# A two-layer gated-linear-attention and latent-attention trunk: x laid out transposed, its norm moved onto the products, and two projections in 512-column blocks

## The chip, the cores and the metric

One Trainium2 chip, one core. The metric is the device time of one execution of the whole program in microseconds (us). Two kernels are compared by the median of several executions on the same chip; one more execution of each is run under the hardware profiler, and its trace is what this document reads.

The engines are named as the profile names them: PE is the matrix engine (PEld its weight loads), DVE the vector engine, ACT the scalar engine, POOL the general one, SP the engine whose queue issues most of the transfers.

## What is computed

512 positions of width 2048 in float32 pass through two layers. Only the parts at the edges of the change are given.

```python
def rms_norm(x, g, eps):                       # over the last axis
    return x * rsqrt(mean(x * x) + eps) * g

def layer0(x):                                 # gated linear attention, 4 heads
    h = rms_norm(x, pre_norm)
    q, k, v, gate, gk_low = split(h @ w_in)    # 1024, 1024, 2048, 2048, 16 columns
    log_a = log_sigmoid(gk_low @ w_gk2 + b_gk) / 16
    o = chunked_scan(q, k, v, log_a)           # o is then normed per head
    return x + rms_norm((rms_norm(o, g) * silu(gate)) @ w_out, post_norm)

def layer1(x):                                 # latent attention, 16 heads
    h = rms_norm(x, pre_norm)
    c_q, c_kv, k_rope, gate = split(h @ w_in)  # 512, 512, 64, 2048 columns
    ...                                        # c_q and c_kv are normed, projected, attended
    return x + rms_norm((attention * silu(gate)) @ w_out, post_norm)
```

## The kernel before

**Numbers.** Every large product is made from three products of rounded parts: an operand is split into a high part (`..._hi`, rounded by ACT or DVE) and the rest (`..._lo`, by DVE), and `mm3` (L123) issues hi·hi, lo·hi and hi·lo into one accumulator. So each weight chunk goes through a load (`chunk_load`, SP's queue), a split (`chunk_split`) and the products. Where a gain of a norm belongs to the layer's input, the split multiplies the weights by it: per 128 weight rows one ACT instruction (L118) and one DVE instruction (L119).

**Tiles.** The 512 positions are four row tiles `s` of 128, the 2048 inputs 16 tiles `k`. `act_hi` and `act_lo` hold the normed input with the inputs on the partitions. In `block_t` the weights are the stationary operand and the 512 positions stream; in `block_s` (through `part_s`) a 128x128 tile of the activations is stationary and the weight columns stream, 256 or 512 of them per product.

**The start** (`start`, L224). x comes in rows, four tiles of 128 positions. For each tile: sums of squares on ACT, the norm's factor, the row times the factor on DVE (L330), sixteen 128x128 transposes on PE in four groups (L333), the split into `act_hi` and `act_lo` (L174, L175). The first head's values are made in two passes of 256 columns: the first inside `start`, row tile by row tile with weights that stay, the second in `gla` (L346). Then `gk_low` (L378), the decays, and the blocks of q, k, gate and v of each head.

**Between the layers** (`between`, L611) each row tile of the first output is normed, added to x, stored, normed again and transposed by the same `rows_to_act`. The first latent, c_q, is also made in two passes of 256 columns. For the first, weights of 14 of the 16 tiles `k` are split ahead (`cq_ahead`, L688) and those of the last two in `mla` (L649); so work for PE is there as each row tile becomes ready.

**Order.** The program is written as above, and a scheduler with a model of its own moves instructions on each engine; every engine then works through its list in order. Transfers of SP's queue start in order, and each buffer waits for its last reader: three raw weight buffers, four split ones, two accumulators for transposes (`ps_t`).

Of the kernel before, what the change touches and what calls it, by code (L numbers as in the profile page):

```python
# [49 lines left out]
R_BGK, R_GON, R_GQA, R_GKV, R_PRE = 0, 8, 12, 16, 20  # L50
NROWS = 36
# [19 lines left out]
class Trunk:  # L71
# [152 lines left out]
    def start(self):  # L224

        nc, a, cp = self.nc, self.a, self.cp
        xs = a["x"][0]
        xt = [self.slot(f"g{s}", [P, D], F32, f"x{s}") for s in range(ST)]
        rows = self.tmp([KT, P], F32, "gain_rows")
        cf = cp.tile([P, P + 1], F32, name="cf")  # L230
        for g in range(4):
            c = slice(g * 512, (g + 1) * 512)
            nc.sync.dma_start(xt[0][:, c], xs[0:P, c])
            if g == 0:
                nc.scalar.dma_start(cf, a["consts"])
                nc.scalar.dma_start(rows, a["l0_pre_norm"].rearrange("(r c) -> r c", c=P))
        self.ident, self.invf = cf[:, 0:P], cf[:, P:P + 1]
        self.eps = cp.tile([P, 1], F32, name="eps")
        nc.vector.memset(self.eps, EPS)
        self.junk = cp.tile([P, 512], BF16, name="junk")  # L240
        pt = self.pss.tile([P, 512], F32, tag="sc", name="gain_t")
        nc.tensor.transpose(pt[:, 0:KT], rows, self.ident[0:KT, 0:KT])
        self.g_in = cp.tile([P, KT], F32, name="g_in0")
        nc.vector.tensor_copy(self.g_in, pt[:, 0:KT])
        w = a["l0_gla_w_in"]
        load = lambda i: self.chunk_load(w, 4 * i, 4, [(GV0, 256)])
        raws = [load(0)]
        nc.sync.dma_start(xt[1], xs[P:2 * P, :])
        raws.append(load(1))
        nc.sync.dma_start(xt[2], xs[2 * P:3 * P, :])  # L250
        raws.append(load(2))
        ws = []
        self.v_ps = [self.acc(f"v_acc{s}", s == 3) for s in range(ST)]
        for s in range(ST):
            parts = self.st.tile([P, 4], F32, tag="parts", name="parts", bufs=2)
            for g in range(4):
                self.sumsq(xt[s][:, g * 512:(g + 1) * 512], parts[:, g:g + 1])
            rstd = self.rstd_of(self.total(parts, "x_ssq"), D, "x_rstd")
            self.rows_to_act(s, xt[s], rstd)
            for i in range(4):  # L260
                if s == 0:
                    if i == 3:
                        raws.append(load(3))
                        nc.sync.dma_start(xt[3], xs[3 * P:4 * P, :])
                    ws.append(self.chunk_split(raws[i], 4 * i, self.g_in, hi_on=nc.vector if i % 2 else None))
                self.part_s(s, 4 * i, ws[i], self.v_ps, slice(0, 256), self.act_hi, self.act_lo, KT)

    def constants(self):
# [11 lines left out]
        rows = self.tmp([P, P], F32, "rows")  # L280
        for r0, name in ((R_BGK, "l0_gla_b_gk"), (R_GON, "l0_gla_g_onorm"),
                         (R_GQA, "l1_mla_g_qa"), (R_GKV, "l1_mla_g_kva"), (R_PRE, "l1_pre_norm")):
            n = a[name].shape[0] // P
            q.dma_start(rows[r0:r0 + n, :], a[name].rearrange("(r c) -> r c", c=P))
        self.ones = cp.tile([P, P], F32, name="ones")
        nc.gpsimd.memset(self.ones, 1.0)
# [3 lines left out]
        pt = self.pst.tile([P, 512], F32, tag="pt", name="gcols")  # L290
        nc.tensor.transpose(pt[:, 0:NROWS], rows[0:NROWS, :], self.ident[0:NROWS, 0:NROWS])
        self.gcol = cp.tile([P, NROWS], F32, name="gcol")
        nc.vector.tensor_copy(self.gcol, pt[:, 0:NROWS])
        with self.tc.issue_after(self.last_norm.ins):
            self.trig(posi, self.invf)
# [43 lines left out]
    def gla(self):  # L339
# [3 lines left out]
        self.vh, self.vl, self.sg = None, None, [None] * GH  # L343
        self.constants()
        self.v_begin()
        self.block_s(w, GV0 + 256, 256, 256, self.v_ps, hi, lo, KT, evac=self.v_evac, gain=self.g_in)  # L346
# [3 lines left out]
        for h in range(GH):  # L350
# [3 lines left out]
            if h:  # L354
                ps = [self.acc(f"v_acc{s}", s == 3) for s in range(ST)]
                self.v_begin()
                self.block_s(w, GV0 + h * GDV, 512, 0, ps, hi, lo, KT, evac=self.v_evac, gain=self.g_in)
# [17 lines left out]
    def v_evac(self, s, ps):  # L375
        self.split_from(ps, self.vh[s], self.vl[s])

    def gk_low(self):  # L378
        nc, v, a = self.nc, self.nc.vector, self.a
        raw = self.tmp([P, KT, 2 * GRANK], F32, "gkl_raw")  # L380
        sc = raw[:, :, GRANK:]
        raw = raw[:, :, 0:GRANK]
        nc.gpsimd.dma_start(raw, a["l0_gla_w_in"][:, GL0:GL0 + GRANK].rearrange("(k p) n -> p k n", p=P))

        wl = self.slot("g1", [P, KT, 3 * GRANK], FR, "gkl_w")
        nc.gpsimd.memset(wl[:, :, GRANK:2 * GRANK].bitcast(F32), 0.0)
        v.tensor_tensor(sc, raw, self.g_in[:, :, None].to_broadcast([P, KT, GRANK]), ALU.mult)
        nc.scalar.copy(wl[:, :, 0:GRANK], sc)
# [254 lines left out]
    def mla(self):  # L643
# [286 lines left out]
```

## Time and profile before

| | us |
|---|---|
| median of 3 executions | 1505.87 (1505.53 to 1507.59) |
| the profiled execution | 1507.5 |
| its span, first to last instruction | 1505.7 |
| PE busy in the span | 1485.8 |
| DVE busy | 742.5 |
| ACT busy | 657.1 |

The span is what the trace covers; 1.8 us of the execution lie around it. A matmul's record lasts longer than the distance to the next one, because matmuls overlap; what a stream of them takes is read from the distances between starts. "Idle before" gives how long an engine stood still ahead of an instruction, and what it waited for. An idle engine costs nothing where another one sets the end.

### The profile page before, as it was taken

The numbers are of one execution on the slowest core, as the hardware profiler recorded it, in microseconds if no ns is written. First come the engines' busy times: TensorE is split into PE (matmuls) and PEld (weight loads), VectorE is DVE, ScalarE is ACT, GpSimd is POOL, SyncE is SP. The second block draws the span as 40 slices with busy tenths as digits, with TensorE's granted clock in tenths as the row PEclk, the third lists the DMA queues.
The fourth block names the chain that finished last, engine by engine and source line by source line (L and its number), as shares of the span: only waits on it lengthen the run. The fifth ranks groups of instructions, "written<-read, shape, count | busy, mean of one in ns | idle before, by whom it ended". The sixth has DMA issues, their size and how long they took to land.

```text
span 1505.7 us, 19208 instructions
## 1 busy us (share of the span) xinstructions
PE 1485.8 (99%) x7490; PEld 1266.6 (84%) x7490; DVE 742.5 (49%) x1337; ACT 657.1 (44%) x1250; POOL 35.0 (2%) x72
## 2 busy tenths in 40 slices
PE   7999999999999999999999999999999999999998
PEld 6988888888888888888889888888888899888886
DVE  6544653355436445434355443333577677853234
ACT  6542642254225424333244443344566667742221
POOL 2100000000000000100011000000000000000000
PEclk9999999999999999999999999999999999999999
DMA  6423223322331323434252333333222111234223
GB/s 222 122 71 98 71 87 95 101 82 80 90 110 57 98 84 119 134 111 134 91 188 92 101 98 98 98 99 91 74 74 74 50 50 55 83 126 168 98 91 119
DMA packets 113867, 149.91 MB, mean 100 GB/s; under 512 B 17580, under 2 KB 66976, under 8 KB 112368
## 3 DMA queue, kind: packets, MB, share of 16 engines
q1 hardware_dynamic: 110176, 136.86, 29.9%
q0 software_dynamic: 3424, 11.75, 2.4%
q8 instruction: 58, 0.95, 0.3%
q14 instruction: 33, 0.27, 0.1%
q10 hardware_dynamic: 176, 0.07, 0.0%
HBM read 140.08 MB, written 8.59 MB: 99 GB/s over the span
## 4 chain that ended last, share of the span: by engine, by line
PE 95%; DVE 2%; ACT 1%; DMA 1%; issue 0%; SPq 0%; DVEq 0%; ACTq 0%
PE acc L125 11%; PE acc L127 11%; PE acc L126 11%; PE yo_acc L125 8%; PE yo_acc L126 8%; PE yo_acc L127 8%; PE v_acc L127 5%; PE v_acc L125 5%; PE v_acc L126 5%; PE o_t L127 1%; PE o_t L126 1%; PE q_acc L127 1%; PE q_acc L126 1%; PE q_acc L125 1%; PE o_t L125 1%; PE pt L882 1%
## 5 line engine op out<-in xcount | busy, mean ns | idle before, releaser
L125 PE MATMUL acc<-act_hi,w_hi 128*128 128x512 f32 x768 | 299.7, 390 | 0.0
L126 PE MATMUL acc<-act_hi,w_lo 128*128 128x512 f32 x768 | 299.2, 390 | 0.0
L127 PE MATMUL acc<-act_lo,w_hi 128*128 128x512 f32 x768 | 298.9, 391 | 0.0
L119 DVE SCALAR_TENSOR_TENSOR w_lo<-w_raw,g_in,w_hi 128x512 fp32r<-128x512 f32 (+1 forms) x208 | 139.7, 707 | 206.7 <-ACT w_hi L118 206.6
L118 ACT ACTIVATE w_hi<-w_raw,g_in 128x512 fp32r<-128x512 f32 (+1 forms) x200 | 128.1, 689 | 242.9 <-PE acc L127 166.6
L127 PEld LDWEIGHTS acc<-act_lo,w_hi 128*128 128x128 f32 x768 | 144.2, 188 | 30.7 <-issue 0.7
L125 PEld LDWEIGHTS acc<-act_hi,w_hi 128*128 128x128 f32 x768 | 144.2, 188 | 30.4 <-issue 0.7
L126 PEld LDWEIGHTS acc<-act_hi,w_lo 128*128 128x128 f32 x768 | 144.3, 188 | 29.8
L111 DVE TENSOR_TENSOR w_lo<-w_raw,w_hi 128x1024 fp32r<-128x1024 f32 x64 | 78.4, 1225 | 166.7 <-ACT w_hi L110 166.6
L110 ACT CAST w_hi<-w_raw 128x1024 fp32r<-128x1024 f32 x64 | 67.3, 1051 | 168.4 <-PE yo_acc L126 156.8
L125 PE MATMUL yo_acc<-w_hi,act_hi 128*128 128x512 f32 x352 | 137.5, 391 | 0.0
L126 PE MATMUL yo_acc<-w_hi,act_lo 128*128 128x512 f32 x352 | 137.1, 390 | 0.0
L127 PE MATMUL yo_acc<-w_lo,act_hi 128*128 128x512 f32 x352 | 137.1, 391 | 0.0
L119 DVE SCALAR_TENSOR_TENSOR w_lo<-w_raw,gcol,w_hi 128x512 fp32r<-128x512 f32 (+1 forms) x98 | 64.6, 699 | 106.1 <-ACT w_hi L118 105.9
L126 PE MATMUL v_acc<-w_hi,act_lo 128*128 128x512 f32 (+1 forms) x320 | 112.2, 352 | 0.0
L118 ACT ACTIVATE w_hi<-w_raw,gcol 128x512 fp32r<-128x512 f32 (+1 forms) x98 | 61.4, 677 | 115.5 <-PE acc L127 83.8
L125 PE MATMUL v_acc<-w_hi,act_hi 128*128 128x512 f32 (+1 forms) x320 | 111.5, 351 | 0.2 <-ACT act_hi L174 0.2
L127 PE MATMUL v_acc<-w_lo,act_hi 128*128 128x512 f32 (+1 forms) x320 | 110.7, 350 | 0.0
L127 PEld LDWEIGHTS yo_acc<-w_lo,act_hi 128*128 128x128 f32 x352 | 66.1, 188 | 14.0 <-issue 0.2
L125 PEld LDWEIGHTS yo_acc<-w_hi,act_hi 128*128 128x128 f32 x352 | 66.1, 188 | 13.8 <-issue 0.2
L126 PEld LDWEIGHTS yo_acc<-w_hi,act_lo 128*128 128x128 f32 x352 | 66.1, 188 | 13.4
L125 PEld LDWEIGHTS v_acc<-w_hi,act_hi 128*128 128x128 f32 x320 | 61.4, 192 | 8.0 <-ACT act_hi L174 0.6
(300 smaller groups left out, 2688.9 us busy)
## 6 DMA issues: line engine op xcount, KB each, us to landing
w_raw<-in_l_gla_w_in_dram SPq DMA_DIRECT2D x64, 512.0 KB, 3.7
w_raw<-in_l_mla_w_in_dram SPq DMA_DIRECT2D x47, 512.0 KB, 3.7
w_raw<-in_l_gla_w_in_dram SPq DMA_DIRECT2D x64, 256.0 KB, 3.0
w_raw<-in_l_gla_w_out_dram SPq DMA_DIRECT2D x32, 512.0 KB, 3.7
w_raw<-in_l_mla_w_out_dram SPq DMA_DIRECT2D x32, 512.0 KB, 3.6
pw_raw<-in_l_mla_w_kvb_dram SPq DMA_DIRECT2D x64, 128.0 KB, 2.3
xo<-in_x_dram POOLq DMA_DIRECT2D x16, 256.0 KB, 6.0
x1d<-yo SPq DMA_DIRECT2D x4, 1024.0 KB, 5.8
```

Of the source, the lines that this page charges most:

```text
L110: nc.scalar.copy(hi, raw)
L111: nc.vector.tensor_tensor(lo, raw, hi.bitcast(F32), ALU.subtract)
L118: nc.scalar.activation(hi[:, kk, :], raw[:, kk, :], AF.Copy, scale=g)
L119: nc.vector.scalar_tensor_tensor(lo[:, kk, :], raw[:, kk, :], g, hi[:, kk, :].bitcast(F32), ALU.mult, ALU.subtract)
L125: t.matmul(out, lh, rh, start=start, stop=False)
L126: t.matmul(out, ll, rh, start=False, stop=False)
L127: t.matmul(out, lh, rl, start=False, stop=stop)
L882: te.transpose(pt[:, o:o + P], probs[i][:, j * P:(j + 1) * P], self.ident)
```

## The change

Host side, x is given a second time, transposed (`xt`, inputs by positions), and the six small gain vectors as one 128x52 array `gains`. In the kernel:

- `start` loads `xt` by tiles `k` beside the first head's value weights in 512 columns. x times its gain is split straight into `act_hi` and `act_lo` (`x_split`); the factor of the norm is left out there. Sums of squares are collected per position over the tiles `k` in `x_ssq`; four narrow products and one 512-column product with ones (`x_norm`) make the factors, per row tile (`rcol`) and along the free axis (`rrow`).
- The weights of layer 0 are split without a gain. The factor is applied to the products: to v in `v_evac`, to q and k in `qk_block`, to the gate in `silu`, to `gk_low`'s 16 rows.
- Five products of zeros (`zeros`) go to PE ahead of everything else.
- c_q is made in one pass of 512 columns: seven tiles `k` split ahead, the eighth in `mla`, the other eight as a block.
- The transposes of gains and small vectors go; `restart` and the scratch of `gk_low` change places.

```diff
@@ start
-        xt = [self.slot(f"g{s}", [P, D], F32, f"x{s}") for s in range(ST)]
...
-        load = lambda i: self.chunk_load(w, 4 * i, 4, [(GV0, 256)])
...
-        for s in range(ST):
...
-            self.rows_to_act(s, xt[s], rstd)
-            for i in range(4):
...
-                self.part_s(s, 4 * i, ws[i], self.v_ps, slice(0, 256), self.act_hi, self.act_lo, KT)
+        self.gcol = cp.tile([P, NCOLS], F32, name="gcol")
+        nc.scalar.dma_start(self.gcol, a["gains"])
+        load_x(0, 1)
+        raws = [self.wp.tile([P, 2, 512], F32, tag="raw", name="w_raw", bufs=3)]
+        for k in range(2):
+            nc.sync.dma_start(raws[0][:, k, :], w[k * P:(k + 1) * P, GV0:GV0 + 512])
+            if k == 0:
+                load_x(1, 1)
...
+        v.memset(self.junk, 0.0)
+        pz = self.pss.tile([P, 512], F32, tag="sc", name="zeros")
+        for _ in range(5):
+            nc.tensor.matmul(pz, self.junk[:, 0:P], self.junk, start=True, stop=True)
...
+        for k0 in range(0, KT, 2):
+            if k0:
+                load_x(k0, 2)
+                raws.append(self.chunk_load(w, k0, 2, [(GV0, 512)]))
+            x = xs[k0 // 4][:, k0 % 4:k0 % 4 + 2, :]
+            if k0:
+                self.x_split(k0, 2, x)
+                wt = self.chunk_split(raws[-1])
...
+            for i in range(2):
...
+                    nc.scalar.activation(sq, x[:, i, :], AF.Square)
+                    v.tensor_tensor(ssq, ssq, sq, ALU.add)
...
+            if k0 + 2 == KT:
+                self.x_norm(ssq)
+            for s in range(ST):
...
+                    self.part_s(s, k0, wt, ps, slice(0, 512), self.act_hi, self.act_lo, KT)
+
+    def x_split(self, k0, nk, x):
+        for i in range(nk):
+            k = k0 + i
+            g = self.gcol[:, R_IN + k:R_IN + k + 1]
+            self.nc.scalar.activation(self.act_hi[:, k, :], x[:, i, :], AF.Copy, scale=g)
+            self.nc.vector.scalar_tensor_tensor(self.act_lo[:, k, :], x[:, i, :], g,
+                                                self.act_hi[:, k, :].bitcast(F32),
+                                                ALU.mult, ALU.subtract)
+
+    def x_norm(self, ssq):
...
+        for s in range(ST):
+            nc.tensor.matmul(pc[:, s:s + 1], ssq[:, s * P:(s + 1) * P], self.ones[:, 0:1],
+                             start=True, stop=True)
...
+        self.norm_mm = nc.tensor.matmul(pn, self.ones, ssq, start=True, stop=True)
@@ constants
-        with self.tc.issue_after(self.last_norm.ins):
+        with self.tc.issue_after(self.last_evac.ins):
             self.trig(posi, self.invf)
@@ gla
-        self.block_s(w, GV0 + 256, 256, 256, self.v_ps, hi, lo, KT, evac=self.v_evac, gain=self.g_in)
@@ qk_block
+            n = self.tmp([P, S], F32, "qk")
+            v.tensor_tensor(n, ps, self.rrow, ALU.mult)
@@ silu
+        if r is not None:
+            nc.vector.tensor_tensor(g, ps, r, ALU.mult)
+            ps = g
@@ mla
-        self.cq_w.append(self.chunk(w, KT - 2, 2, [(MQ0, 256)], self.g_in))
+        self.cq_w.append(self.chunk(w, KT // 2 - 1, 1, [(MQ0, 512)], self.g_in))
         for s in range(ST):
             for i, wt in enumerate(self.cq_w):
-                self.part_s(s, 2 * i, wt, ps, slice(0, 256), hi, lo, KT)
-        self.block_s(w, MQ0 + 256, 256, 256, ps, hi, lo, KT, evac=self.latent_evac, gain=self.g_in)
+                self.part_s(s, i, wt, ps, slice(0, 512), hi, lo, KT)
+        self.block_s(w, MQ0, 512, 0, ps, hi, lo, KT, evac=self.latent_evac, gain=self.g_in,
+                     ks=(KT // 2, KT))
```

**PE at the start.** The list before opens with the transposes of gains and of the first rows (`xn_t`), and only then takes the first products.

```order
L242 MATMUL gain_t<-cf,gain_rows 128x16
L333 MATMUL xn_t<-cf,xn 128x128 x8
L125 MATMUL v_acc_109<-w_hi,act_hi 128x256
L333 MATMUL xn_t<-cf,xn 128x128 x4
L126 MATMUL v_acc_109<-w_hi,act_lo 128x256
L127 MATMUL v_acc_109<-w_lo,act_hi 128x256
```

The changed list opens with the zeros and goes straight to the products of tile `k` = 0, for the four row tiles (accumulators 108 to 111) in turn:

```order
L255 LDWEIGHTS junk
L255 MATMUL zeros<-junk 128x512
L125 MATMUL v_acc_108<-w_hi,act_hi 128x512
L125 MATMUL v_acc_109<-w_hi,act_hi 128x512
L125 MATMUL v_acc_110<-w_hi,act_hi 128x512
L125 MATMUL v_acc_111<-w_hi,act_hi 128x512
L126 MATMUL v_acc_108<-w_hi,act_lo 128x512
```

All transposes of x are gone from this place, and the columns per product are 512.

**SP's queue at the start.** Before: the first rows of x in four pieces, then weights and rows in turn.

```order
L233 DMA x_82<-in_x_dram 128x512 x4
L98 DMA w_raw<-in_l_gla_w_in_dram 128x4x256
L248 DMA x_83<-in_x_dram 128x2048
L98 DMA w_raw<-in_l_gla_w_in_dram 128x4x256
L250 DMA x_84<-in_x_dram 128x2048
```

Now: one tile `k` of x, its weights, the next of each, and from there two tiles at a time.

```order
L232 DMA xt_82<-in_xt_dram 128x512
L240 DMA w_raw<-in_l_gla_w_in_dram 128x512
L232 DMA xt_82<-in_xt_dram 128x512
L240 DMA w_raw<-in_l_gla_w_in_dram 128x512
L232 DMA xt_82<-in_xt_dram 128x2x512
L98 DMA w_raw<-in_l_gla_w_in_dram 128x2x512
```

The first product needs two transfers of 256 KB where it needed six.

**PE between the layers,** around the third row tile's first transposes (the `xn_t` row of each list; accumulators 6063 and 5586 are the second row tile of c_q). Before, twelve narrow products of the weights split ahead (`cqw`) stand between the second row tile's last transposes and this one:

```order
L125 MATMUL cq_acc_6063<-cqw_hi,act_hi 128x256
L126 MATMUL cq_acc_6063<-cqw_hi,act_lo 128x256
L127 MATMUL cq_acc_6063<-cqw_lo,act_hi 128x256
L125 MATMUL cq_acc_6063<-cqw_hi,act_hi 128x256
L333 MATMUL xn_t<-cf,xn 128x128 x4
L126 MATMUL cq_acc_6063<-cqw_hi,act_lo 128x256
L127 MATMUL cq_acc_6063<-cqw_lo,act_hi 128x256
```

Now twelve wide ones, the last four of them with the block's own weights (`w_hi`, `w_lo`):

```order
L127 MATMUL cq_acc_5586<-cqw_lo,act_hi 128x512
L125 MATMUL cq_acc_5586<-w_hi,act_hi 128x512
L126 MATMUL cq_acc_5586<-w_hi,act_lo 128x512
L127 MATMUL cq_acc_5586<-w_lo,act_hi 128x512
L125 MATMUL cq_acc_5586<-w_hi,act_hi 128x512
L374 MATMUL xn_t<-cf,xn 128x128 x4
L126 MATMUL cq_acc_5586<-w_hi,act_lo 128x512
L127 MATMUL cq_acc_5586<-w_lo,act_hi 128x512
```

The same number of products stands there, each with twice the columns. From the first c_q product to these transposes the changed list has 67 products and six groups of four transposes.

## Rows read from the trace of the kernel before

**Rows 1.** The page's first part: span; busy us, share, instructions of each engine.

```profile
span 1505.7 us, 19208 instructions
PE 1485.8 (99%) x7490; PEld 1266.6 (84%) x7490; DVE 742.5 (49%) x1337; ACT 657.1 (44%) x1250; POOL 35.0 (2%) x72
```

**Rows 2.** Waits of PE, whole span: us in total, times, longest us.

```profile
PE xn_t L333 <- DVE xn L330: 4.1, 1, 4.1
PE xn_t L333 <- DVE act_lo L175: 2.9, 3, 2.0
```

**Rows 3.** PE in time, the start: start us, us, what [idle before, releaser].

```profile
9.57 1.97 PE L333 MATMUL xn_t<-cf,xn 128*128 128x128 f32 x8 [4.15 <-DVE xn L330]
...
15.13 0.41 PE L126 MATMUL v_acc<-w_hi,act_lo 128*128 128x256 f32 x1
15.34 0.41 PE L127 MATMUL v_acc<-w_lo,act_hi 128*128 128x256 f32 x1
...
18.86 0.28 PE L125 MATMUL v_acc<-w_hi,act_hi 128*128 128x256 f32 x1
18.98 0.28 PE L126 MATMUL v_acc<-w_hi,act_lo 128*128 128x256 f32 x1
...
68.91 0.39 PE L393 MATMUL gkl_acc<-act_hi,gkl_w 128*48 128x512 f32 x1
```

**Rows 4.** PE in time: 46 wide products of layer 0's output, 22 narrow of c_q.

```profile
769.77 0.39 PE L125 MATMUL yo_acc<-w_hi,act_hi 128*128 128x512 f32 x1
...
779.97 0.39 PE L125 MATMUL yo_acc<-w_hi,act_hi 128*128 128x512 f32 x1
...
837.72 0.28 PE L127 MATMUL cq_acc<-w_lo,act_hi 128*128 128x256 f32 x1
...
840.24 0.28 PE L127 MATMUL cq_acc<-w_lo,act_hi 128*128 128x256 f32 x1
```

**Rows 5.** PE in time, one group of four transposes between two products.

```profile
24.32 0.29 PE L125 MATMUL v_acc<-w_hi,act_hi 128*128 128x256 f32 x1
24.44 0.60 PE L333 MATMUL xn_t<-cf,xn 128*128 128x128 f32 x4
...
25.00 0.28 PE L127 MATMUL v_acc<-w_lo,act_hi 128*128 128x256 f32 x1
```

**Rows 6.** PE between the layers; then busy us by engine, granted clock (PEclk) of 800-810.

```profile
784.26 0.28 PE L125 MATMUL cq_acc<-cqw_hi,act_hi 128*128 128x256 f32 x1
...
802.32 0.66 PE L333 MATMUL xn_t<-cf,xn 128*128 128x128 f32 x4 [1.96 <-DVE act_lo L175]
...
804.18 0.42 PE L127 MATMUL cq_acc<-cqw_lo,act_hi 128*128 128x256 f32 x1
804.39 0.41 PE L125 MATMUL cq_acc<-cqw_hi,act_hi 128*128 128x256 f32 x1
800.00:810.00 10.00, 8.04 (x56) 7.84 (x55) 6.47 (x13) 4.76 (x13) 0.00 (x0) 0.83 0.26 107
```

**Rows 7.** ACT in time, first and third piece of x; the stretch 10-20 (last: GB/s).

```profile
4.52 0.63 ACT L185 ACTIVATE junk<-x 128x512 bf16<-128x512 f32 x1 [2.50 <-DMA x<-in_x_dram]
...
6.76 0.63 ACT L185 ACTIVATE junk<-x 128x512 bf16<-128x512 f32 x1 [0.68 <-DMA x<-in_x_dram]
...
10.00:20.00 10.00, 9.18 (x46) 8.33 (x44) 8.87 (x23) 8.56 (x25) 0.21 (x1) 1.00 1.03 376
```

**Rows 8.** Groups by line and shape: busy us, mean ns of one, idle before.

```profile
L119 DVE SCALAR_TENSOR_TENSOR w_lo<-w_raw,g_in,w_hi 128x512 fp32r<-128x512 f32 x176 | 125.7, 748 | 205.6 <-ACT w_hi L118 205.6
L111 DVE TENSOR_TENSOR w_lo<-w_raw,w_hi 128x1024 fp32r<-128x1024 f32 x64 | 78.4, 1225 | 166.7 <-ACT w_hi L110 166.6
L546 DVE TENSOR_TENSOR o_ssq<-o_ssq,o_sq 128x512 f32<-128x512 f32 x12 | 8.3, 690 | 16.6 <-ACT o_sq L545 16.6
L118 ACT ACTIVATE w_hi<-w_raw,g_in 128x512 fp32r<-128x512 f32 x176 | 117.9, 716 | 239.6 <-PE acc L127 166.6 <-PE v_acc L126 62.7 <-issue 10.3
L549 PE MATMUL o_norm<-o_ssq,ones 128*128 128x512 f32 x8 | 4.1, 592 | 0.0
```

More of the change, by code (lines that the diff above doesn't have):

```diff
@@ L224, in start @@
     def start(self):
-        nc, a, cp = self.nc, self.a, self.cp
-        xs = a["x"][0]
-        xt = [self.slot(f"g{s}", [P, D], F32, f"x{s}") for s in range(ST)]
-        rows = self.tmp([KT, P], F32, "gain_rows")
-        cf = cp.tile([P, P + 1], F32, name="cf")
[L231 to L236, printed above, removed]
+        nc, v, a, cp = self.nc, self.nc.vector, self.a, self.cp
@@ L242, in start @@
[L242 to L245, printed above, removed]
-        load = lambda i: self.chunk_load(w, 4 * i, 4, [(GV0, 256)])
[L247 to L253, printed above, removed]
@@ L254, in start @@
-        for s in range(ST):
[L255 to L258, printed above, removed]
-            self.rows_to_act(s, xt[s], rstd)
-            for i in range(4):
[L261 to L265, printed above, removed]
-                self.part_s(s, 4 * i, ws[i], self.v_ps, slice(0, 256), self.act_hi, self.act_lo, KT)
+        self.ones = cp.tile([P, P], F32, name="ones")
@@ new lines, in start @@
+        nc.gpsimd.memset(self.ones, 1.0)
+        v.memset(self.junk, 0.0)
+        pz = self.pss.tile([P, 512], F32, tag="sc", name="zeros")
+        for _ in range(5):
+            nc.tensor.matmul(pz, self.junk[:, 0:P], self.junk, start=True, stop=True)
+        ssq = self.slot("b24", [P, S], F32, "x_ssq")
+        ps = [self.acc(f"v_acc{s}", s == 3) for s in range(ST)]
+        self.v_begin()
+        for k0 in range(0, KT, 2):
[6 more added lines that the diff above has]
+                wt = self.chunk_split(raws[-1])
+            else:
+                hi = self.wp.tile([P, 2, 512], FR, tag="w_hi", name="w_hi", bufs=4)
+                lo = self.wp.tile([P, 2, 512], FR, tag="w_lo", name="w_lo", bufs=4)
+                for k in range(2):
+                    self.x_split(k, 1, x[:, k:k + 1, :])
+                    v.tensor_copy(hi[:, k, :], raws[0][:, k, :])
+                    v.tensor_tensor(lo[:, k, :], raws[0][:, k, :], hi[:, k, :].bitcast(F32), ALU.subtract)
+                wt = hi, lo
+            for i in range(2):
+                if k0 + i == 0:
+                    nc.scalar.activation(ssq, x[:, 0, :], AF.Square)
+                else:
+                    sq = self.tmp([P, S], F32, "x_sq")
+                    nc.scalar.activation(sq, x[:, i, :], AF.Square)
+                    v.tensor_tensor(ssq, ssq, sq, ALU.add)
+            if k0 == 10:
+                self.gk_weights()
+            if k0 + 2 == KT:
+                self.x_norm(ssq)
+            for s in range(ST):
+                if k0 + 2 == KT:
+                    with self.tc.issue_after(self.norm_mm.ins):
+                        self.part_s(s, k0, wt, ps, slice(0, 512), self.act_hi, self.act_lo, KT)
+                    self.v_evac(s, ps[s])
+                else:
+                    self.part_s(s, k0, wt, ps, slice(0, 512), self.act_hi, self.act_lo, KT)
@@ L279, in constants @@
         self.m_past, self.m_future = cm[:, 0:P], cm[:, P:2 * P]
[L280 to L286, printed above, removed]
         big = cp.tile([P, 1], F32, name="big")
@@ L356, in gla @@
                 self.v_begin()
-                self.block_s(w, GV0 + h * GDV, 512, 0, ps, hi, lo, KT, evac=self.v_evac, gain=self.g_in)
+                self.block_s(w, GV0 + h * GDV, 512, 0, ps, hi, lo, KT, evac=self.v_evac)
             else:
@@ L910, in _constants, with _laid_out @@
     return {"consts": cf, "masks": masks}
+def _laid_out(given):
+    names = ("l0_gla_b_gk", "l0_gla_g_onorm", "l1_mla_g_qa", "l1_mla_g_kva", "l1_pre_norm", "l0_pre_norm")
+    rows = np.concatenate([given[n].reshape(-1, P) for n in names])
+    return {"xt": np.ascontiguousarray(given["x"][0].T), "gains": np.ascontiguousarray(rows.T)}
 def kernel(**inputs):
@@ L920 @@
     given.update(_constants())
+    given.update(_laid_out(given))
     arrays, a = {}, {}
```

87 lines of the change are left out of this document (50 added, 37 removed).

## Prediction

> **What bounds the kernel now.** The first part of the page comes first: PE is busy for 1485.8 of 1505.7 us [rows 1]. Some 20 us are left for any change that only removes waits. But a busy PE is not a PE at its best, so the second view is PE's instructions in order of time, where the distance from one start to the next says what a product takes. The third is the list of PE's waits, which says where the idle time lies.
>
> Products of 512 columns start 0.2267 us apart: 46 of them from 769.77 to 779.97, 45 distances in 10.20 us. Products of 256 columns start 0.120 apart: 22 from 837.72 to 840.24 [rows 4]. Two narrow ones take 0.240, one wide one 0.2267. PE has no gap in either stretch, so a narrow product pays for its weight load.
>
> A group of four transposes costs 0.44 us: from 24.32 to 25.00 lie two narrow products (0.24) and the group [rows 5].
>
> The start is the place where PE does little. It first stands until 9.57, after a last wait of 4.15 for the first normed row tile, and reaches gk_low at 68.91 [rows 3]. In between lie 384 narrow products (16 tiles k, four row tiles, three products each, two passes), 46.1 us, and 16 groups of transposes, 7.0; together 53.1 of 59.3. Most of the other 6.2 is the clock: at 15.13 narrow products start 0.21 apart, from 18.86 on 0.12 [rows 3]. 256 columns in 0.213 us is the lower of PE's two levels, 1.2 GHz. Between the layers the same spacing, 0.21, is seen at 804, after PE had stood still for 1.96 us; the granted clock of the ten microseconds from 800 is 0.83, that is 3.4 us at half speed [rows 6]. Of the two waits for transposes, 4.1 lies at the start, and of the 2.9 all but 0.9 is this one [rows 2].
>
> **The start, step by step.** After the change PE reaches gk_low after its first product's wait, 192 wide products, the norm's products, and what the low clock costs.
>
> The first product needs one tile of x and one of weights, 256 KB each, the first and second in SP's queue. Before, the first piece of x, of the same size and place, lets ACT go at 4.52, and the third at 6.76 [rows 7]; I put the second at 5.4. ACT then makes a square (as the squares of x in rows 7, 0.63) and the copy with the gain (0.716 [rows 8]): 5.9. DVE rounds the weights beside that. I take 6.0; if the weights land as late as the third piece, it is 7.5. The zeros lie in PE's idle time before that and cost nothing; if they raise the clock early, that is a gain that I don't count.
>
> 192 × 0.2267 = 43.5 us. The norm adds one product of float32 with ones, two records of at most 592 ns [rows 8], 1.2 us, and four narrow ones, taken as a group of transposes, 0.44: 1.7 together.
>
> The low clock: the trace has it from the first transposes at 9.57 to shortly before 18.86, some 9.0 us, with gaps in PE's work at the beginning, and for 3.4 us between the layers. A stretch at half speed loses (1 − 0.2267/0.4267) = 0.47 of its length, so between 1.6 and 4.2 us; I take the middle, 2.9.
>
> Sum: 6.0 + 43.5 + 1.7 + 2.9 = 54.1 instead of 68.91: **14.8 us gained** (12.0 to 16.2 with the bounds of both). gk_low itself has the same 32 products.
>
> What must keep up beside it: a pair of tiles k is 1 MB of loads, and PE takes 24 × 0.2267 = 5.4 us for it. The stretch 10-20 moved 376 GB/s [rows 7], so 1 MB in 2.8 us. DVE has per pair two splits of x (0.748), two sums (0.690) and one weight split (1.225) [rows 8]: 4.1 us. All below 5.4, so the loads and DVE gain on PE pair by pair. The next to be late would be the trigonometry, now behind the last values; the decays that wait for it are needed only after a q and k block of 192 × 0.2267 = 43.5 us.
>
> **Layer 0 otherwise.** 32 multiplications by the factor come to DVE (16 for q and k, 16 for the gate; 0.690 each, 22 us). 176 splits of 0.748 become 88 of 1.225: 131.6 to 107.8 us, 24 less [rows 8]. Each evacuation still frees its accumulator after one instruction, for q and k instead of after two. The list of waits has none of PE in this layer after the start, so I put all of it at zero; if it costs, it is at the eight block ends of q, k and gate, 0.69 each.
>
> **c_q.** 384 narrow products become 192 wide: 192 × 0.0133 = 2.6 us. Then the stall. PE reaches the third row tile's first transposes at 802.32 − 1.96 = 800.36, 16.1 us after the first c_q product at 784.26 [rows 6], and waits for DVE to empty a transpose buffer, 18.1 us after. In the changed list 67 wide products and six groups of transposes come before that place: 15.2 + 2.6 = 17.8 us. DVE's own list there is the same work in nearly the same order (its weight splits are 512 instead of 256 columns), so I keep 18.1: the stall shrinks from 1.96 to 0.3, and the low clock after it should not come, 0.47 × 3.4 = 1.6. Together 2.6 + 1.7 + 1.6 = **5.9 us**; 2.6 if the stall stays as it is.
>
> **A rule against this.** The rows say that width itself is worth 2.6 us at each of the two places. The Trainium skill, "TensorE: Matmul & The Clock Gate", section "Back-to-back issue gap", gives the distance of isolated products as columns by 2.4 GHz plus 2.5 ns, 109 and 216 ns. By it a pair of narrow ones costs 2.5 ns more than one wide one, 0.5 us at each place, and the sum would be 4.2 us smaller. The rows have 0.120 and 0.2267 in streams without a gap, and the sum goes by them.
>
> **The sum.** 14.8 + 5.9 = 20.7 us. The profiled execution took 1507.5, so its like would take 1486.8. The median of the runs shown is 1505.87, 1.6 below; against it the forecast is 1505.9 − 20.7 = **1485.2 us**.
>
> **Rivals.**
> - *The stall between the layers stays.* DVE's emptying of the buffer stands in its queue behind four sums of the last row tile; if these come later by what PE now does longer, the 1.96 and the low clock remain. Against it: nothing that DVE waits for there is a c_q product. Time: 1485.2 + 3.3 = 1488.5. Chance 0.2.
> - *The loads are late at the start.* x and the weights now come interleaved on one queue, and the second pair may not be there when the first is done; three to five microseconds of waits at the first pairs, 1488 to 1490. For it: the third 256 KB landed 2.2 us after the first, where 376 GB/s would make it 1.4 [rows 7]. Against: the low clock stretches the first pair to as much as 24 × 0.427 = 10 us. Chance 0.13.
> - *Time is given back in layer 0.* The added multiplication holds up each of the eight block ends: 5.5 us, 1490.7. Against: PE never waits at a block end now. Chance 0.05.
> - *Width is worth nothing,* since columns alone set the time and something else held the narrow products at 0.120: 5.1 us less, 1490.3. Against: both streams are dense [rows 4]. Chance 0.02. The Trainium skill's gap rule, named above, stands close to this one.
> - *The clock stays low.* If the pairs come in bursts with waits between, PE may run the whole first block at 1.2 GHz, as it did after gaps in rows 3 and 6. All 192 products at 0.427 take 81.9 us: 6.0 + 81.9 + 3.4 = 91.3, 22.4 later than now, minus 5.9: 1522, **slower**. It decides from about 118 cold products on, where 0.2 us each have eaten 20.7 + 2.9. Against: loads and splits need half to three quarters of PE's time per pair. Chance 0.03.
> - Half of that, or a mix that ends within 0.2% of now (about what a measurement of this kernel can tell from no change): 0.02.
>
> **How the numbers follow.** The forecast holds with 0.55. Its own range: 12.0 to 16.2 at the start and 5.5 to 6.2 for c_q give 1483.5 to 1488.4. The range to 80% takes in the stall that stays, and the late loads, up to 1491; below, norm products at half my price and a clock raised by the zeros, to 1481. Left out are the clock, the mix, and parts of the smaller ones, under 0.2. Faster 0.95, within 0.2% 0.02, slower 0.03.
>
> **What would show it.** First wide product near 6.0, spaced 0.427 for some microseconds and 0.227 after; no wait of PE over 1 us until gk_low at about 54. Between the layers c_q products 0.227 apart, no wait near 2 us and no stretch with a granted clock below 1. Wrong would be: waits of PE for w_hi or act_hi inside the first block, 0.427 beyond 15 us, a PE wait at the head of a q, k or gate block, or again the wait for act_lo between the layers.

## The result, and the profile after

The changed kernel takes 1489.99 us (median of four executions, 1489.72 to 1490.51) against 1505.7 of the kernel before on the same chip: a ratio of 0.9891 with a 95% interval of 0.9875 to 0.9907. It is 15.7 us faster. The forecast was 1485.2 with a range of 1481 to 1491: the sign and the range hold, and the point is 4.8 us too low. The profiled execution took 1489.72, its span is 1487.9.

The page's first table, beside [rows 1]:

```profile
PE 1474.9 (99%) x7055; PEld 1236.5 (83%) x7055; DVE 738.3 (50%) x1230; ACT 625.7 (42%) x1109; POOL 32.5 (2%) x67
```

PE is still the bound, with 10.9 us less work and 6.9 us less idle time (13.0 instead of 19.9). The list of PE's waits, which answers to [rows 2]:

```profile
PE v_acc L125 <- DVE w_hi L272: 2.9, 1, 2.9
PE zeros L255 <- DVE junk L252: 1.2, 1, 1.2
PE lat_t L768 <- DVE lat_row L760: 0.7, 1, 0.7
PE k_acc L125 <- DVE qr_t L868: 0.3, 1, 0.3
PE v_acc L125 <- ACT w_hi L110: 0.2, 1, 0.2
PE v_acc L127 <- DVE w_lo L111: 0.2, 1, 0.2
PE cq_acc L125 <- ACT act_hi L174: 0.2, 1, 0.2
```

Both waits for transposes are gone, the 4.1 at the start and the 2.0 between the layers. New are the wait for the first weights (2.9), three short ones for later weights and for the second row tile's `act_hi` (0.2 each), and `lat_t` (0.7), which the forecast had not named. The zeros' own wait (1.2) lies in time in which PE had nothing else to do. Between 55 and 764 us, all the rest of layer 0, the list of waits is empty.

PE in order of time at the start, which answers to [rows 3] (start, duration, what, count, and in brackets the idle time before and its releaser):

```profile
6.39 2.04 PE L125 MATMUL v_acc<-w_hi,act_hi 128*128 128x512 f32 x4 [2.85 <-DVE w_hi L272]
8.24 1.91 PE L126 MATMUL v_acc<-w_hi,act_lo 128*128 128x512 f32 x4
9.94 1.82 PE L127 MATMUL v_acc<-w_lo,act_hi 128*128 128x512 f32 x4
11.60 1.10 PE L125 MATMUL v_acc<-w_hi,act_hi 128*128 128x512 f32 x4
12.54 1.08 PE L126 MATMUL v_acc<-w_hi,act_lo 128*128 128x512 f32 x4
...
25.61 0.50 PE L125 MATMUL v_acc<-w_hi,act_hi 128*128 128x512 f32 x1 [0.19 <-ACT w_hi L110]
...
48.01 0.95 PE L309 MATMUL x_norm_c<-ones,x_ssq 128*128 128x1 f32 x8
48.82 1.10 PE L312 MATMUL x_norm<-x_ssq,ones 128*128 128x512 f32 x2
...
49.99 0.40 PE L126 MATMUL v_acc<-w_hi,act_lo 128*128 128x512 f32 x1
...
55.25 0.40 PE L436 MATMUL gkl_acc<-act_hi,gkl_w 128*48 128x512 f32 x1
```

The first wide product starts at 6.39. Groups of four start 1.66 to 1.85 us apart until 11.60, the lower of PE's two levels, and 0.92 to 0.94 after it, 0.23 each, the upper one. The profile's granted clock doesn't show this stretch: it reads 1.00 from 0 to 10 and from 10 to 20 us, as it does from 10 to 20 in [rows 7]. So at the start the level is read from the spacing alone. The norm puts 49.99 − 0.23 − 48.01 = 1.75 us between two products. gk_low starts at 55.25, where it started at 68.91 [rows 3].

The other place is c_q, which answers to [rows 6]. PE at its beginning, where the stall was, and at its end:

```profile
770.65 0.39 PE L125 MATMUL cq_acc<-cqw_hi,act_hi 128*128 128x512 f32 x1
...
821.08 0.39 PE L127 MATMUL cq_acc<-w_lo,act_hi 128*128 128x512 f32 x1
822.14 0.41 PE L768 MATMUL lat_t<-cf,lat_row 128*128 128x128 f32 x2 [0.67 <-DVE lat_row L760]
822.31 0.48 PE L125 MATMUL ckv_acc<-w_hi,act_hi 128*128 128x512 f32 x1
```

From the first c_q product to the first of c_kv it is 51.7 us; in the trace of before, 56.2 (784.26 to 840.50). So the two traces are 13.6 us apart when c_q begins and 4.6 more when it ends, and lose 0.4 after that: 17.8 between the spans. The medians are only 15.7 apart. Which part of c_q's 4.6 is real was the first question.

### The profile page after: what moved, and what is told of

Same layout as the page of the kernel before. It is cut to its first block, busy times and chain, and to the rows that moved or that the text cites. A ratio compares the mean times of both kernels' runs of the same rounds, so it can differ in the third digit from the quotient of the medians.

```text
span 1487.9 us, 18076 instructions
## 1 busy us (share of the span) xinstructions
PE 1474.9 (99%) x7055; PEld 1236.5 (83%) x7055; DVE 738.3 (50%) x1230; ACT 625.7 (42%) x1109; POOL 32.5 (2%) x67
## 4 chain that ended last, share of the span: by engine, by line
PE 95%; DMA 2%; DVE 2%; ACT 1%; issue 1%; SPq 0%; DVEq 0%; ACTq 0%
PE acc L127 11%; PE acc L126 11%; PE acc L125 11%; PE yo_acc L125 8%; PE yo_acc L126 8%; PE yo_acc L127 8%; PE v_acc L127 5%; PE v_acc L126 5%; PE v_acc L125 4%; PE o_t L127 1%; PE o_t L126 1%; PE q_acc L126 1%; PE q_acc L127 1%; PE q_acc L125 1%; PE o_t L125 1%; PE pt L932 1%
## 5 line engine op out<-in xcount | busy, mean ns | idle before, releaser
L111 DVE TENSOR_TENSOR w_lo<-w_raw,w_hi 128x1024 fp32r<-128x1024 f32 x159 | 194.3, 1223 | 379.3 <-ACT w_hi L110 378.9
L110 ACT CAST w_hi<-w_raw 128x1024 fp32r<-128x1024 f32 x159 | 167.3, 1053 | 428.4 <-PE acc L127 186.7
L119 DVE SCALAR_TENSOR_TENSOR w_lo<-w_raw,gcol,w_hi 128x512 fp32r<-128x512 f32 x89 | 63.2, 747 | 101.0 <-ACT w_hi L118 100.9
L118 ACT ACTIVATE w_hi<-w_raw,gcol 128x512 fp32r<-128x512 f32 x89 | 59.8, 716 | 111.6 <-PE acc L127 83.8
L125 PE MATMUL v_acc<-w_hi,act_hi 128*128 128x512 f32 x256 | 100.2, 396 | 3.0 <-DVE w_hi L272 2.9
L126 PE MATMUL v_acc<-w_hi,act_lo 128*128 128x512 f32 x256 | 99.5, 393 | 0.0
L127 PE MATMUL v_acc<-w_lo,act_hi 128*128 128x512 f32 x256 | 97.1, 393 | 0.2 <-DVE w_lo L111 0.2
L126 PE MATMUL yo_acc<-w_hi,y_lo 128*128 128x512 f32 x160 | 62.5, 391 | 0.0
L125 PE MATMUL yo_acc<-w_hi,y_hi 128*128 128x512 f32 x160 | 62.4, 391 | 0.0
L127 PE MATMUL yo_acc<-w_lo,y_hi 128*128 128x512 f32 x160 | 61.8, 390 | 0.0
```

Source lines behind the costliest of these rows:

```text
L110: nc.scalar.copy(hi, raw)
L111: nc.vector.tensor_tensor(lo, raw, hi.bitcast(F32), ALU.subtract)
L118: nc.scalar.activation(hi[:, kk, :], raw[:, kk, :], AF.Copy, scale=g)
L119: nc.vector.scalar_tensor_tensor(lo[:, kk, :], raw[:, kk, :], g, hi[:, kk, :].bitcast(F32), ALU.mult, ALU.subtract)
L125: t.matmul(out, lh, rh, start=start, stop=False)
L126: t.matmul(out, ll, rh, start=False, stop=False)
```

## The experiments

Two theories. **A**: the low clock between the layers [rows 6] is not in every execution of the kernel before, so a term of the forecast was never there in the median; the rest of the gap is small things at both places. **B**: the traces are right as they stand, and the shortfall has its cause elsewhere.

**before_again**: the kernel before, without an edit.

> The kernel before, unchanged. The traces of the two kernels lie 17.8 us apart, their medians 15.7. Theory A: the low clock after the stall between the layers (1.6 us of loss) comes in some executions of this kernel only, so most runs give 1505.5 to 1505.9 and a few 1507.5; a profiled run near 1505.6 shows the 1.96 us wait before the third row tile's transposes but no granted clock below 0.95 between 800 and 810, and c_q products 0.120 apart right after it. Theory B: the stretch of low clock is in every execution, the profile of before is only one slow sample of everything, and a profiled run near 1505.6 differs from the first by a little everywhere.

Measured: 1506.31 (1505.7 to 1506.93, 11 executions) beside 1505.83 of the 21 others on this chip; the profiled one took 1506.93. PE at the place of [rows 6], then the ten microseconds from 800 (busy us by engine, granted clock, DMA share, GB/s):

```profile
803.23 0.66 PE L333 MATMUL xn_t<-cf,xn 128*128 128x128 f32 x4 [2.05 <-DVE act_lo L175]
...
804.20 0.28 PE L127 MATMUL cq_acc<-cqw_lo,act_hi 128*128 128x256 f32 x1
804.32 0.28 PE L125 MATMUL cq_acc<-cqw_hi,act_hi 128*128 128x256 f32 x1
```

```profile
800.00:810.00 10.00, 7.95 (x68) 7.75 (x68) 7.40 (x14) 5.43 (x14) 0.00 (x0) 1.00 0.26 107
```

The wait is there, 2.05 us, the granted clock is 1.00 where it was 0.83, and the products behind the wait are 0.12 apart where they were 0.21. From these transposes to the third group after them PE takes 6.76 us (803.23 to 809.99) where it took 8.29 (802.32 to 810.61): the low clock cost 1.5 in that execution, close to the 1.6 of the forecast. From c_q to c_kv it is 55.1 us instead of 56.2; the other 0.4 were lost ahead of the transposes. So the stall belongs to the kernel, and the low clock after it does not come with every execution. The time is not the 1505.6 that the expectation spoke of: the start of this execution was 0.5 later. Theory A on the clock holds. How often it comes was not counted; of the 21 others on this chip three took 1507.42 to 1508.61 and all the rest less than 1506.7, but no trace shows what the three did.

**cq_alone**: only c_q and its split ahead are changed.

```diff
-        self.block_s(w, MQ0 + 256, 256, 256, ps, hi, lo, KT, evac=self.latent_evac, gain=self.g_in)
+        self.block_s(w, MQ0, 512, 0, ps, hi, lo, KT, evac=self.latent_evac, gain=self.g_in,
+                     ks=(KT // 2, KT))
...
-        for k0, nk in ((0, 4), (4, 4), (8, 4), (12, 2)):
+        for k0, nk in ((0, 2), (2, 2), (4, 2), (6, 1)):
```

> Only the part on c_q is made: 512-column blocks, seven tiles split ahead; the start stays as before. Theory A (width 2.6, the stall 1.7, a new wait at the end of c_q of about 0.9, and a low clock that before has only sometimes): 2.6 + 1.7 - 0.9 = 3.4 less, 1502.3. Theory B (traces as they are): 4.5 less, 1501.2. If width is worth what isolated products would say, 0.5: 1504.4.

Measured: 1503.15, 2.7 less than 1505.83 (ratio 0.9981, 0.9973 to 0.999). It is 0.85 above A's figure, 1.95 above B's, and not half of the 5.9 forecast. The stall is gone, and the wait for `lat_row` is there:

```profile
PE lat_t L719 <- DVE lat_row L711: 0.8, 1, 0.8
```

**start_alone**: the changed kernel with c_q in two passes, the same diff backwards.

> The changed start and layer 0, with c_q in two passes of 256 columns as before. Theory A: 13.7 less by the traces up to layer 0's output, 1492.0, with the stall between the layers back at about 2 us. Theory B: all of the shortfall against the forecast lies at the start, 11.5 less, 1494.2.

Measured: 1492.08 (1491.82 to 1492.75), 13.75 less than before, as A has it. PE between the layers and the ten microseconds around it:

```profile
786.79 0.28 PE L125 MATMUL cq_acc<-cqw_hi,act_hi 128*128 128x256 f32 x1
788.68 0.66 PE L374 MATMUL xn_t<-cf,xn 128*128 128x128 f32 x4 [1.60 <-DVE act_lo L175]
```

```profile
780.00:790.00 10.00, 8.39 (x71) 8.19 (x71) 8.72 (x19) 8.14 (x25) 0.00 (x0) 1.00 0.57 210
```

The stall is back and again the clock stays full (the products behind it are 0.12 apart). The two parts add up: 13.75 and 2.7 make 16.4, 13.75 and the 2.1 between this kernel and the changed one make 15.8, where 15.7 was measured for both.

**no_zeros**: the changed kernel with `range(0)` for `range(5)`.

> The changed kernel without the five products of zeros. They end at 3.5 us and PE stands still for 2.85 us after them. Theory A: that gap undoes them, they are worth nothing, 1490.0 (within 0.4), and the first wide products are 0.43 apart until about 11.6 as with them. Rival: they bring the full clock forward, and without them the low clock lasts to 13 or 14, 1 us more, 1491.

Measured: 1489.97 against 1489.99. PE's first groups:

```profile
6.40 2.05 PE L125 MATMUL v_acc<-w_hi,act_hi 128*128 128x512 f32 x4 [6.40 <-DVE w_hi L272]
...
11.37 1.09 PE L125 MATMUL v_acc<-w_hi,act_hi 128*128 128x512 f32 x4
```

Without the five products the first pair is as slow as with them, until 11.37 instead of 11.60. They do nothing for the time.

**twelve_zeros**: `range(12)`.

> Twelve products of zeros instead of five, so that PE stands still for no more than a few tenths of a us before the first wide product. Theory A (what undoes the five is the gap of 2.85 us, and the clock rises after some microseconds of work without a gap): the first wide products are 0.23 apart from 7 or 8 us on instead of 11.6, up to 2.2 less, 1488. Theory B (zeros don't count as work): 0.43 until 11.6 as now, 1490.0. Theory C: the clock rises, but the loads of the first pairs are then what PE waits for, and less than 1 us is left.

Measured: 1490.18 (1489.94 to 1490.75). PE's rows:

```profile
1.23 4.68 PE L255 MATMUL zeros<-junk 128*128 128x512 bf16 x12 [1.23 <-DVE junk L252]
6.76 1.17 PE L125 MATMUL v_acc<-w_hi,act_hi 128*128 128x512 f32 x4 [0.86 <-DVE w_hi L272]
7.77 1.07 PE L126 MATMUL v_acc<-w_hi,act_lo 128*128 128x512 f32 x4
...
13.81 0.50 PE L125 MATMUL v_acc<-w_hi,act_hi 128*128 128x512 f32 x1 [1.35 <-ACT w_hi L110]
...
26.02 0.50 PE L125 MATMUL v_acc<-w_hi,act_hi 128*128 128x512 f32 x1 [1.03 <-ACT w_hi L110]
```

Theory C: the full clock is there from the first wide product (groups 0.9 to 1.0 apart), and every microsecond of it goes into waits for the weights' splits, 1.35 and 1.03. gk_low starts at 55.7, later than the 55.25 above. So at the start two limits lie over each other, the low clock and the supply of weights, and to lift the first alone is worth nothing. A run that leaves the start as it is says the same. In the trace of no_factor (below) the upper level came sooner and the second twelve products began at 10.65, 0.95 sooner than in the changed kernel's; a longer wait took it back.

```profile
10.65 1.08 PE L125 MATMUL v_acc<-w_hi,act_hi 128*128 128x512 f32 x4
...
25.51 0.50 PE L125 MATMUL v_acc<-w_hi,act_hi 128*128 128x512 f32 x1 [1.02 <-ACT w_hi L110]
```

That product starts at 25.51 here, at 25.61 in the changed kernel and at 26.02 with twelve zeros, each time right behind ACT's split; gk_low follows at 55.15, 55.25 and 55.67. start_alone, ckv_first and ckv_other_acc wait 1.01 at the same place.

**v_narrow**: the first head's values as pairs of 256-column products, nothing else moved.

```diff
+            for j in range(2):
+                c = slice(256 * j, 256 * j + 256)
+                self.mm3(ps[s][:, c], self.act_hi[:, k, r], self.act_lo[:, k, r],
+                         w[0][:, kk, c], w[1][:, kk, c],
+                         k == 0 and j == 0, k == KT - 1 and j == 1)
```

> The changed kernel, with each 512-column product of the first head's values made as two of 256 columns, one after the other; loads, splits and order stay. Theory (a narrow product pays for its weight load, 2 x 0.120 against 0.2267): 192 pairs, 2.6 more, less what the cold first products give back, 1492.3 to 1492.6, and products 0.120 apart from 16 us on. Rival (width is worth 2.5 ns a pair, as isolated products would say): 0.5 more, 1490.5. Second rival: the loads set the pace of the first pairs, so a slower PE costs less than 2.6.

Measured: 1492.53 (1492.5 to 1492.69), 2.54 more. Both kernels in the stretch 30 to 40 us (busy PE, PEld, DVE, ACT, POOL, then granted clock), first v_narrow, then the changed kernel:

```profile
30.00:40.00 10.00, 10.00 (x86) 10.00 (x85) 9.85 (x17) 5.07 (x8) 3.69 (x8) 1.00 0.75 231
```

```profile
30.00:40.00 10.00, 10.00 (x46) 8.29 (x45) 9.21 (x15) 5.28 (x8) 3.35 (x8) 1.00 0.70 221
```

The term of 2.6 is shown. In the narrow stream the weight loads are busy for all of the ten microseconds, in the wide one for 8.29; that fits a narrow product that is paced by its weight load, but no run changed the loads alone. The Trainium skill, "TensorE: Matmul & The Clock Gate", section "Back-to-back issue gap", has a formula for isolated products by which this would have been 0.5, and says itself that the formula counts too little for few columns, since it leaves out the weight load. The 2.54 agrees with that; the formula was no rule against the rows.

**no_factor**: the multiplications of q, k and the gate by the factor are left out (`n = ps`, and `silu` without `r`).

> The changed kernel without the 32 multiplications of q, k and the gate by the norm's factor, which this kernel leaves out. Theory (hidden, the term was put at zero): within 0.4 of 1490.0. Rival (they hold up the eight block ends, 0.69 each): 5.5 less, 1484.5.

Measured: 1489.98. DVE's busy time falls from 738.3 to 723.9 and the end doesn't move. The term of zero for layer 0 is shown.

**ckv_first**: the first chunk of c_kv's products ahead of the transposes of c_q's rows.

```diff
-        self.latent_end(cq, R_GQA)
...
-        self.block_s(w, MKV0, 512, 0, ps, hi, lo, KT, evac=self.latent_evac, gain=self.g_in)
+        self.block_s(w, MKV0, 512, 0, ps, hi, lo, KT, gain=self.g_in, ks=(0, 2))
+        self.latent_end(cq, R_GQA)
+        ckv = self.latent_begin(8, "ckv")
+        self.block_s(w, MKV0, 512, 0, ps, hi, lo, KT, evac=self.latent_evac, gain=self.g_in, ks=(2, KT))
```

> The changed kernel, with the first chunk of c_kv's products (24 wide ones, 5.4 us) ahead of the transposes of c_q's rows. Theory: the wait of 0.67 for lat_row with the 0.4 around it at the end of c_q goes, 0.8 to 1.0 less, 1489.1. Rival: the rows are evacuated later too, since DVE and ACT have c_kv's weights to split in between, and the wait comes back behind the chunk, 1490.0.

Measured: 1490.24 (1489.34 to 1490.87), no gain. PE at the seam:

```profile
820.95 0.39 PE L127 MATMUL cq_acc<-w_lo,act_hi 128*128 128x512 f32 x1
822.40 0.50 PE L125 MATMUL ckv_acc<-w_hi,act_hi 128*128 128x512 f32 x1 [1.07 <-DVE lat_row L761]
```

A miss for both: the wait stayed in its place and changed its victim. c_kv's first product needs c_q's first accumulator, which the same `lat_row` empties.

**ckv_other_acc**: the same, with the first two row tiles of c_kv in banks that attention uses later.

```diff
-        ps = [self.acc(f"ckv_acc{s}", s == 3) for s in range(ST)]
+        ps = ([self.pss.tile([P, 512], F32, tag="sc", name="ckv_acc") for _ in range(2)]
+              + [self.acc(f"ckv_acc{s}") for s in (2, 3)])
```

> The changed kernel, with the first chunk of c_kv's products ahead of the transposes of c_q's rows, and the first two row tiles of c_kv in the two banks that attention uses later, so that they wait for no row of c_q. With the first chunk ahead alone the wait of 1.07 had gone to c_kv's first product, which needed c_q's first accumulator. Theory: now 0.8 to 1.2 less, 1489.0, c_kv's first product 0.23 to 0.4 behind c_q's last. Rival: the wait moves on to the third row tile's accumulator or to the weights of c_kv, 1490.0.

Measured: 1489.1 (1488.81 to 1489.22), 0.9 less. PE at the seam:

```profile
821.17 0.39 PE L127 MATMUL cq_acc<-w_lo,act_hi 128*128 128x512 f32 x1
821.40 0.39 PE L125 MATMUL ckv_acc<-w_hi,act_hi 128*128 128x512 f32 x1
```

The two lie 0.23 apart. From c_q to c_kv it is 50.8 us instead of 51.7. So the new wait costs 0.9 in the changed kernel.

**paced_loads** and **paced_twelve_zeros**: from the seventh tile on, x is loaded behind the weights of the pair before; the second with `range(12)` too.

```diff
+                    with self.tc.issue_after(self.last_load.ins):
+                        load_x(k0, 2)
```

> The changed kernel, with the loads of x from the seventh tile on held behind the weights of the pair before, so that SP's queue carries x and weights by turns; in the changed kernel four pairs of x run ahead and the weights stand behind 2 MB. Theory (the weights set the pace of the first pairs, and the low clock until 11.6 only fills time in which PE would wait): nearly nothing, since PE only waits 0.2 to 1.0 there now: 1489.4 to 1490. Rival (the low clock alone set it): 1490.0 with the same small waits.

> The loads of x and weights by turns and twelve products of zeros. Theory: the zeros give the full clock from the first wide product on (seen with twelve zeros), and with the weights no longer late the 2.4 of low clock stay gained: c_q and all behind it 2 to 3 earlier, 1487.5. Rival (the bytes themselves are late: 24 x 0.2267 = 5.4 us of work per MB asked from a queue that moved some 200 GB/s until 6.5 us): waits of 1 to 2 us at the first pairs stay and the time is 1489.5 to 1490.

Measured: 1488.7 (1488.22 to 1489.67) and 1488.45 (1487.91 to 1489.39). In the changed kernel ACT's list has four pairs of x between two splits of weights, 9 us apart; with the loads by turns (the kernel with twelve zeros) the splits start at 12.16, 15.38, 18.59 and 21.81. The changed kernel's ACT:

```profile
15.54 1.03 ACT L110 CAST w_hi<-w_raw 128x1024 fp32r<-128x1024 f32 x1
16.47 1.33 ACT L299 ACTIVATE act_hi<-xt,gcol 128x512 fp32r<-128x512 f32 x2
...
23.29 1.32 ACT L299 ACTIVATE act_hi<-xt,gcol 128x512 fp32r<-128x512 f32 x2
24.52 1.03 ACT L110 CAST w_hi<-w_raw 128x1024 fp32r<-128x1024 f32 x1
```

The weights of the split at 24.52 had landed at 20.75 (those of the fourth pair in the queue); the other 3.8 us are ACT's list. By turns alone gk_low starts at 54.59, with the zeros at 53.30, with one wait of 0.87 at 13.24 left. In the traces that is 0.66 and 1.95 of the start. In the medians it is 1.3 and 1.5. Part of it is given back between the layers: in the first, c_q waited 0.67 for its second row tile's `act_hi` and was at c_kv only 0.07 ahead, within the profiled execution, which was also the longest of its four; in the second it waited 0.63 there and 1.0 for `lat_row`, and 1.1 of the 1.95 were left. Both expectations were missed by 0.7 to 1.0 us, the first on the good side, the second on the bad. Between the two of them, 0.25 lies within their spread, so what the zeros add to the paced loads stays open.

**combined**: paced loads, ten zeros, c_kv in other banks, and the constants and gk_low's second weights moved behind the first three pairs.

```diff
-        nc.scalar.dma_start(cf, a["consts"])
...
+            if k0 == 6:
+                self.sixth = self.last_load
+                with self.tc.issue_after(self.sixth.ins):
+                    nc.sync.dma_start(cf, a["consts"])
...
-                nc.gpsimd.dma_start(t[r, :], a["l0_gla_w_gk2"][:, c])
+                with self.tc.issue_after(self.sixth.ins):
+                    nc.sync.dma_start(t[r, :], a["l0_gla_w_gk2"][:, c])
```

> The changed kernel with x and weights by turns on SP's queue, ten products of zeros, the first chunk of c_kv ahead in the two other banks, and the small early transfers (the constants and gk_low's second weights, 64 KB and 192 KB in short rows) moved behind the first three pairs on SP's queue. Theory: the parts lie at different places and add: 1.6 by paced loads with zeros, 0.9 by c_kv, 1487.5; and if the small transfers hold up the first weights, these land at 4.5 to 5 instead of 5.8 and the first wide product starts 0.8 to 1.3 sooner, 1486.5. Rival for the last part: the first weights land at 5.8 as before, and the time is 1487.5. Rival for the whole: an earlier start is lost again between the layers, where PE waits for the first row tile (0.6 to 0.7 with paced loads, 0.2 without), 1488.

Measured: 1487.01 (1485.87 to 1487.16), ratio to before 0.9866 (0.985 to 0.9883): all four executions lie below all of both kernels, and the median 3.0 below the changed one's. (On this chip the kernel before took 1507.18, on the others 1505.7 to 1506.1, so the 3.0 is rather too small than too large.) PE's waits and its first groups:

```profile
PE zeros L254 <- DVE junk L251: 1.2, 1, 1.2
PE v_acc L125 <- DVE w_hi L279: 0.6, 1, 0.6
...
```

```profile
1.22 4.45 PE L254 MATMUL zeros<-junk 128*128 128x512 bf16 x10 [1.22 <-DVE junk L251]
6.30 2.05 PE L125 MATMUL v_acc<-w_hi,act_hi 128*128 128x512 f32 x4 [0.63 <-DVE w_hi L279]
...
11.01 1.08 PE L125 MATMUL v_acc<-w_hi,act_hi 128*128 128x512 f32 x4
```

The first weights are split at 5.73 instead of 5.82: the small transfers do not hold them up, and that part of the theory falls. gk_low starts at 53.6, with the low clock back until 11.0 but no wait for weights behind it. From c_q to c_kv it is 50.6, so c_kv begins 2.7 sooner than in the changed kernel, 1.6 of it from the start: the parts add, and the start is not lost again between the layers.

## Why the prediction was right, and which terms were off

Most of what it said would show the change did show: spacing of 0.43 and then 0.23, layer 0 without a wait, no stall and no low clock between the layers. The sign "no wait of PE over 1 us until gk_low" held in this trace (0.2) and only just failed in four others with the same start (1.01 and 1.02). And a sign that it had named as wrong, a wait for w_hi inside the first block, is there.

That the range held is in part luck. The sum's own range was 1483.5 to 1488.4, and 1489.99 lies outside it. It was held by the part up to 1491, which was there for a stall that stays and for late loads; the stall did not stay, and the weights were late by 0.2 to 1.0 and not by three to five.

The point missed by 5.0 us of gain (15.7 instead of 20.7), in these terms:

| term | forecast | measured | from |
|---|---|---|---|
| first product | 6.0 | 6.39 | the trace after; DVE has the first weights at 5.82, forecast 5.4 |
| low clock at the start | 2.9 | 2.5 | 12 products in 5.21 us instead of 2.72; most of it PE would have waited (below) |
| norm | 1.7 | 1.75 | the trace after |
| products and waits | 43.5 | 44.6 | what is left up to 55.25; two waits with the slow products around them, 0.9 of it |
| **gained at the start** | 14.8 | 13.7 | start_alone, and 68.91 − 55.25 |
| layer 0 | 0 | 0 | no_factor |
| c_q: width and transposes | 2.6 | 2.0 | what is left of the 2.6 by which c_q is shorter in the trace after than in start_alone's |
| c_q: stall | 1.7 | 1.4 | 1.77 before the transposes in start_alone; now none there, 0.33 at an earlier product |
| c_q: low clock | 1.6 | 0 | before_again, start_alone |
| c_q: wait for `lat_row` | not named | −0.8 to −0.9 | the trace after, ckv_other_acc |
| **gained at c_q** | 5.9 | 2.1 to 2.7 | medians of start_alone and cq_alone |

The step that failed is "the low clock after it should not come, 0.47 × 3.4 = 1.6". The row was read rightly, and its price was right for that execution (1.5). But it is a row of one execution of 1507.5, and the gain was then taken off the median of 1505.87, in whose executions that stretch need not be: neither before_again nor start_alone had it. The text had both times, 1.6 us apart, and did not ask which of its terms was in the one and not in the other.

The second step is in the sum for c_q: it ended with the products and did not follow the last row tiles out. In the kernel before, PE finishes the row tiles 1.44 us apart, twelve narrow products each, and ACT begins with the first 4.1 us ahead of the transposes at 840.36, 0.3 behind the start of that row tile's last product (835.92). In the changed one PE's list finishes them four wide products apart, 0.9. The first one's last product starts at 818.36; ACT begins 1.2 behind that, 1.8 us ahead of the end of the products, because a split of c_kv's weights stands before it in ACT's list. ACT of the kernel before, then of the changed one:

```profile
836.24 0.60 ACT L185 ACTIVATE junk<-cq_acc 128x512 bf16<-128x512 f32 x1 [0.22 <-PE cq_acc L127]
```

```profile
818.30 1.34 ACT L118 ACTIVATE w_hi<-w_raw,gcol 128x512 fp32r<-128x512 f32 x2 [2.48 <-DMA w_raw<-in_l_mla_w_in_dram]
819.55 0.57 ACT L185 ACTIVATE junk<-cq_acc 128x512 bf16<-128x512 f32 x1
...
820.45 0.58 ACT L185 ACTIVATE junk<-cq_acc 128x512 bf16<-128x512 f32 x1
...
821.02 0.19 ACT L181 ACTIVATE lat_rstd<-lat_rstd 128x1 f32<-128x1 f32 x1
```

The second row tile's squares (820.45) even stand ahead of the first one's last factor (821.02). What the shorter distance and what ACT's order gave to the wait, no run took apart. [Rows 2] have no wait at this seam, and that was read as a place without a price.

The third is small: 192 × 0.0133 = 2.6 holds for a dense stream, as in v_narrow (2.54). In c_q some 2.0 came of it. While groups of transposes stand between the products (770.6 to 810.6), the wide ones start 0.231 apart by the median, and 0.227 after that; the narrow ones of start_alone keep 0.120 in both stretches. A group costs 0.44 to 0.45 in either kernel. Why the wide products lose there is not shown.

At the start the sum came out near the trace, but its terms do not simply add. The sentence that "the loads and DVE gain on PE pair by pair" is a further step that failed: it left out ACT, whose list puts four pairs of x ahead of a split of weights, and that split sets when PE goes on at 25.5 to 26.0. The low clock's 2.5 mostly fills time in which PE would have waited: at the full clock the waits for weights are 1.35 and 1.03 (twelve_zeros). The argument against the second rival, that the low clock stretches the first pair, points the right way, but it does not cover the split at 24.5. The rivals of a stall that stays, of width worth nothing, of time given back in layer 0 and of a clock that stays low are all refuted by the rows above.

## What to carry to other kernels

A term that rests on a clock or a wait of one profiled execution is to be held against the spread of the runs before it is taken off their median. Where the products of a block become wider, follow the last evacuations too: how far ahead of the next block they begin, and what stands before them in the evacuating engine's list, tells who waits at the seam, and a chunk put ahead helps only if it needs no accumulator of the block before. At a start, ask what the second limit would be at once: here the low clock lay over the wait for weights; to lift the clock alone was worth nothing, to lead x and weights by turns 1.3 (paced_loads), both 1.5.

## What the runs showed of the hardware

After stalls of nearly one length PE's clock did different things: after 1.96 us it fell (granted 0.83 over ten microseconds, [rows 6]), after 2.05 (before_again) and 1.60 (start_alone) it stayed at 1.00, with the products 0.12 apart.

Idle time before the first product did not by itself decide its clock either. After twelve zeros and a gap of 0.86 us it ran at the upper level from its first group; after ten zeros and a gap of 0.63 the groups were slow until the third (9.85 to 11.01). The records of the zeros tell the two apart: ten took 4.45 us and started 0.43 apart, the lower level, and twelve took 4.68, so the last ones among them were already fast. In paced_twelve_zeros all twelve were slow (5.30), no gap followed, and only the first group was still in part slow (1.24 to the next). Why the level rose when it did was not tried.

A stream of 256-column products keeps the weight loads busy for 10.00 of 10.00 us (v_narrow), one of 512 columns for 8.29.
